# Weights cast to bf16 inside the DMA, in order of first use, with the conditioning projection first and in row form

## The chip, the cores and the metric

The kernel runs on all 8 cores of one Trainium2 chip. Every core does the same program on 2 of the 16 samples and no core talks to another. The metric is device time in microseconds of the slowest core. In code and profiles PE is TensorE, PEld the loading of its stationary operand, DVE is VectorE, ACT is ScalarE, POOL is GpSimd and SP is SyncE.

Such a program has two states. In the slow one the cores of one die, or of both, run at a lower granted TensorE clock and the time is some per cent longer (in one run one die stood at 0.84 and the other at 0.99). Where a number is given "by core", it is the median of the 8 cores of the one execution that was traced.

## The reference, cut to what matters

```python
shift, scale, gate = split(silu(c) @ w_mod + b_mod, 3)      # conditioning: (3, 1024) per sample
h  = rms_norm(x) * g_pre * (1 + scale) + shift              # needed before anything else
xa, ga, q, k, v, gb, gm = split(h @ w_in)                   # 1024 -> 5632
y_a = pool_mixer(xa) * silu(ga)                             # w_branch_a follows
y_b = windowed_attention(rope(q), rope(k), v, k_ctx, v_ctx) * silu(gb)   # w_branch_b follows
merged = sigmoid(gm_a) * (y_a @ w_branch_a) + sigmoid(gm_b) * (y_b @ w_branch_b)
out = x + gate * rms_norm(merged @ w_out) * g_post          # w_out: the last weight of a tile
```

Everything is fp32 in HBM. The kernel computes its large matmuls in bf16. The fp32 weights are 46 MB: 12.6 MB `w_mod`, 23.1 MB `w_in`, 10.5 MB for the two branch matrices and `w_out` (called `w_a`, `w_b`, `w_o` below).

Shift and scale are needed by the first tile's norm. The gate is needed only by the end of a tile.

## The kernel before

All weights stay in SBUF as bf16. A core first loads and converts all of them, then computes the conditioning, then works through 2 x (2 context + 32 latent) tiles of 128 tokens. The two start-up parts each end in a barrier, because their staging memory is used again by what follows.

```python
# part 1: stage every weight in fp32, cast it on DVE and ACT in turn   (5 staging buffers)
def load_cast(dst_ap, src_ap, n, dst_buf, mul_ap=None):
    si = cast_rr["s"] % NS
    E("sp", lambda e: e.dma_start(out=stg[si][:, 0:n], in_=src_ap), ...)              # L300
    if ci == 0:
        E("dve", lambda e: e.tensor_copy(out=dst_ap, in_=stg[si][:, 0:n]), ...)       # L308
    else:
        E("act", lambda e: e.activation(out=dst_ap, in_=stg[si][:, 0:n], func=AF.Copy), ...)  # L310
# ... w_tok, w_feat (= w_in), w_a, w_b, w_o, band and mask tables ...
tr.barrier()

# part 2: conditioning; six blocks of w_mod, [128, 8, 512] fp32 each, two buffers
for blk in range(6):
    if blk < 4:                      # shift, scale: column form, w_mod stationary
        for cc in range(4):
            for k in range(8):
                E("pe", matmul(out=psA[:, ch*4:(ch+1)*4],
                               lhsT=wst[wi][:, k, cc*128:(cc+1)*128], rhs=sc[:, k*4:(k+1)*4]))   # L375
    else:                            # gate: every row of the output is the same gate row
        for j in range(BPC):
            for k in range(8):
                E("pe", matmul(out=pg, lhsT=screp[j][:, k, :], rhs=wst[wi][:, k, :]))            # L384
# ... the gate rows go to a scratch tensor in HBM, 4 KB in one piece each, and come back broadcast ...
tr.barrier()
# part 3: the tiles
```

A helper keeps the order: each engine runs its own instructions strictly in program order, and an instruction waits for the producers of what it reads and the readers of what it overwrites. SP is the engine whose queue issues the DMAs here.

The softmax here doesn't subtract the row's maximum and nothing guards it: scores larger than these inputs give would overflow.

Of the kernel before, what the change touches and what calls it, by code (L numbers as in the profile page):

```python
# [13 lines left out]
D = 1024  # L14
# [4 lines left out]
NEG = -30000.0  # L19
HP = [0, 4, 1, 5, 2, 6, 3, 7, 8, 12, 9, 13, 10, 14, 11, 15]  # L20
# [149 lines left out]
def build_program(L, STOP=0):  # L170
    NT = L // 128
    nc = bass.Bass("TRN2", target_bir_lowering=False)
# [7 lines left out]
    wtok_d = din("w_tok", [D, 3072])  # L180
    wfeat_d = din("w_feat", [D, 2560])
    wa_d = din("w_a", [512, D])
    wb_d = din("w_b", [D, D])
    wout_d = din("w_o", [D, D])
    poolw_d = din("pool_w", [128, 512])
    wmod_d = din("w_mod", [D, 3072])
    bmodT_d = din("b_modT", [128, 16])
    bgate_d = din("b_gate", [1, D])
    gpreT_d = din("g_preT", [128, 8])
    gpost_d = din("g_post", [1, D])  # L190
# [24 lines left out]
    with es:  # L215
        def sb(name, shape, dt, stack=es):
            return stack.enter_context(nc.sbuf_tensor("s_" + name, list(shape), dt))

        Wtok = sb("Wtok", [128, 8, 3072], BF16)
        Wfeat = sb("Wfeat", [128, 8, 2560], BF16)  # L220
        Wa = sb("Wa", [128, 4, D], BF16)
        Wb = sb("Wb", [128, 8, D], BF16)
        Wo = sb("Wo", [128, 8, D], BF16)
# [54 lines left out]
        with ExitStack() as ps_:  # L278
            identf = sb("identf", [128, 128], F32, ps_)
            NS = 5  # L280
            stg = [sb(f"stg{i}", [128, 1536], F32, ps_) for i in range(NS)]
            pscl = sb("pscl", [128, 512], F32, ps_)
            sinkb = sb("sinkb", [128, 16], F32, ps_)

            E("pool", lambda e: e.memset(identf[:], 0.0), writes=[bf("identf")])
            E("pool", lambda e: e.affine_select(out=identf[:], in_=identf[:], pattern=[[-1, 128]],
                                                compare_op=ALU.not_equal, fill=1.0, base=0, channel_multiplier=1),
              reads=[bf("identf")], writes=[bf("identf")])
            E("pool", lambda e: e.tensor_copy(out=ident[:], in_=identf[:]), reads=[bf("identf")], writes=[bf("ident")])
            ld(pscl[:], pscale_d.partition_broadcast(128), "pscl")  # L290
            ld(sinkb[:], sink_d.partition_broadcast(128), "sinkb")

            cast_rr = {"i": 0, "s": 0}

            def load_cast(dst_ap, src_ap, n, dst_buf, mul_ap=None):
                si = cast_rr["s"] % NS
                cast_rr["s"] += 1
                sbuf_ = bf(f"stg{si}")
                s_ = dsem(f"d_stg{si}")
                E("sp", lambda e: e.dma_start(out=stg[si][:, 0:n], in_=src_ap), writes=[sbuf_], dma_sem=s_)  # L300
                if mul_ap is not None:
                    E("dve", lambda e: e.tensor_tensor(out=dst_ap, in0=stg[si][:, 0:n], in1=mul_ap, op=ALU.mult),
                      reads=[sbuf_, bf("pscl")], writes=[dst_buf])
                    return
                ci = cast_rr["i"] % 2
                cast_rr["i"] += 1
                if ci == 0:
                    E("dve", lambda e: e.tensor_copy(out=dst_ap, in_=stg[si][:, 0:n]), reads=[sbuf_], writes=[dst_buf])  # L308
                else:
                    E("act", lambda e: e.activation(out=dst_ap, in_=stg[si][:, 0:n], func=AF.Copy), reads=[sbuf_], writes=[dst_buf])  # L310

            for k in range(8):
                for h in range(2):
                    load_cast(Wtok[:, k, h * 1536:(h + 1) * 1536], wtok_d[k * 128:(k + 1) * 128, h * 1536:(h + 1) * 1536], 1536, bf("Wtok"))
            for k in range(8):
                for h in range(2):
                    load_cast(Wfeat[:, k, h * 1280:(h + 1) * 1280], wfeat_d[k * 128:(k + 1) * 128, h * 1280:(h + 1) * 1280], 1280, bf("Wfeat"))
            for k in range(4):
                load_cast(Wa[:, k, :], wa_d[k * 128:(k + 1) * 128, :], 1024, bf("Wa"))
            for k in range(8):  # L320
                load_cast(Wb[:, k, :], wb_d[k * 128:(k + 1) * 128, :], 1024, bf("Wb"))
            for k in range(8):
                load_cast(Wo[:, k, :], wout_d[k * 128:(k + 1) * 128, :], 1024, bf("Wo"))
            load_cast(view(Wp, 0, [[1, 512]]), poolw_d, 512, bf("Wp"), mul_ap=pscl[:])
            load_cast(view(band, 0, [[1, 1536]]), band_d[:, 0:1536], 1536, bf("band"))
            load_cast(view(band, 1536, [[1, 1024]]), band_d[:, 1536:2560], 1024, bf("band"))
            load_cast(view(maskb, 0, [[1, 256]]), mask_d, 256, bf("maskb"))
            E("act", lambda e: e.activation(out=esink[:], in_=sinkb[:], func=AF.Exp), reads=[bf("sinkb")], writes=[bf("esink")])
            tr.barrier()

        with ExitStack() as ps_:
            wst = [sb(f"wst{i}", [128, 8, 512], F32, ps_) for i in range(2)]
            cT = sb("cT", [128, 32], F32, ps_)
            th = sb("th", [128, 32], F32, ps_)
            sc = sb("sc", [128, 32], F32, ps_)
            screp = [sb(f"screp{j}", [128, 8, 128], F32, ps_) for j in range(BPC)]
            mT = sb("mT", [128, 64], F32, ps_)
            bmodT = sb("bmodT", [128, 16], F32, ps_)
            gpreT = sb("gpreT", [128, 8], F32, ps_)
            bgate = sb("bgate", [128, D], F32, ps_)  # L340
            gpost = sb("gpost", [128, D], F32, ps_)
            gtmp = sb("gtmp", [128, 512], F32, ps_)
            ggt1 = sb("ggt", [128, D], F32, ps_)
            ggt = [ggt1, ggt1]

            ld(cT[:], cT_d, "cT")
            def load_wmod(blk):
                wi = blk % 2
                E("sp", lambda e: e.dma_start(
                    out=wst[wi][:], in_=wmod_d[:, blk * 512:(blk + 1) * 512].rearrange("(k p) n -> p k n", p=128)),  # L350
                  writes=[bf(f"wst{wi}")], dma_sem=dsem(f"d_wst{wi}"))
            load_wmod(0)
            load_wmod(1)
            ld(bmodT[:], bmodT_d, "bmodT")
            ld(gpreT[:], gpreT_d, "gpreT")
            ld(bgate[:], bgate_d.partition_broadcast(128), "bgate")
            ld(gpost[:], gpost_d.partition_broadcast(128), "gpost")

            E("act", lambda e: e.activation(out=th[:], in_=cT[:], func=AF.Tanh, scale=0.5), reads=[bf("cT")], writes=[bf("th")])
            E("dve", lambda e: e.scalar_tensor_tensor(out=sc[:], in0=th[:], scalar=1.0, in1=cT[:], op0=ALU.add, op1=ALU.mult),  # L360
              reads=[bf("th"), bf("cT")], writes=[bf("sc")])
            E("dve", lambda e: e.tensor_scalar_mul(out=sc[:], in0=sc[:], scalar1=0.5), reads=[bf("sc")], writes=[bf("sc")])
            for j in range(BPC):
                E("dve", lambda e, j=j: e.tensor_copy(out=screp[j][:], in_=view(sc, j, [[4, 8], [0, 128]])),
                  reads=[bf("sc")], writes=[bf(f"screp{j}")])

            psA, psAb = next_bank()
            psG = [[next_bank() for nb in range(2)] for j in range(BPC)]
            for blk in range(6):
                wi = blk % 2  # L370
                if blk < 4:
                    for cc in range(4):
                        ch = blk * 4 + cc
                        for k in range(8):
                            E("pe", lambda e, wi=wi, cc=cc, ch=ch, k=k: e.matmul(  # L375
                                out=psA[:, ch * 4:(ch + 1) * 4], lhsT=wst[wi][:, k, cc * 128:(cc + 1) * 128],
                                rhs=sc[:, k * 4:(k + 1) * 4], start=(k == 0), stop=(k == 7)),
                              reads=[bf(f"wst{wi}"), bf("sc")], writes=[psAb], inc=(k == 7))
                else:
                    nb = blk - 4  # L380
                    for j in range(BPC):
                        pg, pgb = psG[j][nb]
                        for k in range(8):
                            E("pe", lambda e, wi=wi, j=j, k=k, pg=pg: e.matmul(  # L384
                                out=pg[:, :], lhsT=screp[j][:, k, :], rhs=wst[wi][:, k, :], start=(k == 0), stop=(k == 7)),
# [557 lines left out]
```

## Time and profile before

| | us |
|---|---|
| median of 4 runs | 2961.94 |
| fast runs | 2960.47, 2961.90, 2961.99 |
| one run in the slow state | 3227.13 |
| traced span of the slowest core | 2960.8 |
| first `w_o` matmul starts, by core | 290.8 (284.6 to 292.9) |
| from there to the end, by core | 2665.1 |

The page of the profile cuts the span into 40 equal slices of 74 us. A digit is the busy share of an engine in tenths; PEclk is the granted TensorE clock in tenths of full speed; DMA is the mean busy share of the core's 16 DMA engines.

```profile
span 2960.8 us, 80701 instructions; the slowest of 8 cores (2948.8 to 2960.8 us)
...
PE   0287999999999999999996999999999999999998
...
PEclk9998999999999999999998999999999999999999
DMA  9840000000000000000001000000000000000000
GB/s 316 252 115 30 32 32 32 17 32 32 32 17 32 32 32 24 25 32 32 32 16 53 17 32 32 20 29 32 32 27 22 32 32 32 17 32 32 32 24 16
```

TensorE is idle in the first slice and busy 90% or more in nearly every slice from the fifth on. The DMA engines are busy mainly at the start. So there is a start of some 300 us and a long TensorE-bound body.

The table of stretches gives, per stretch, the busy time of PE, PEld, DVE, ACT and POOL with their instruction counts, then clock, DMA share and GB/s:

```profile
core 7: us, PE busy (x) PEld busy (x) DVE busy (x) ACT busy (x) POOL busy (x), PEclk, DMA share, GB/s
...
60.00:80.00 20.00, 0.00 (x0) 0.00 (x0) 4.00 (x5) 6.64 (x6) 0.00 (x0) 1.00 1.00 334
...
160.00:180.00 20.00, 20.00 (x96) 20.00 (x95) 0.00 (x0) 0.00 (x0) 0.00 (x0) 1.00 0.59 173
...
200.00:220.00 20.00, 12.09 (x29) 5.04 (x27) 2.08 (x3) 0.00 (x0) 4.15 (x9) 0.85 0.11 27
```

```profile
304.00:346.00 42.00, 39.77 (x497) 27.94 (x496) 20.51 (x62) 18.52 (x36) 8.69 (x8) 1.00 0.10 32
346.00:388.00 42.00, 39.77 (x498) 27.93 (x496) 20.46 (x61) 18.52 (x36) 8.69 (x8) 1.00 0.09 31
```

While weights arrive, the DMA engines are saturated (1.00 at 334 GB/s) and the casts on DVE and ACT take a third of their time at most: they hide under the transfers. During the projection the DMA engines are half idle and TensorE is full. From 304 us on, a tile takes 42 us with 39.8 us of TensorE work. The Trainium skill ("HBM Reference", Specifications) gives about 358 GB/s per core when both cores of a pair are active; this trace shows somewhat less, 334.

The chain of waits, followed back from the end, lists start, length and what was waited for:

```profile
116.42 10.61 DMA s_wst<-w_mod
127.30 54.75 PE pb L375 x256
182.05 30.06 PE pb L384 x64
...
214.51 1.27 DMA gg_scr<-s_ggt
215.86 4.72 DMA s_xt<-ctx
...
294.25 1.89 PE pb L719 x8
```

The start is serial: weights to 115 us, projection to 212, tiles from 216, first output projection (L719, second half of its matmuls) at 294.

### The profile page before, as it was taken

To read this page: it belongs to the slowest core of one execution; us is meant where nothing else is said; L and a number is where in the kernel's file an instruction comes from. 1 tells how busy PE (TensorE), PEld (TensorE's weight loads), DVE (VectorE), ACT (ScalarE), POOL (GpSimd) and SP (SyncE) were. 2 spreads that over 40 slices of the span, in tenths; PEclk is the share of its full clock that TensorE was granted. 3 is DMA by queue.
4 is the path that set the end of the run, shared out by engine and by line. 5 is a ranking of instruction groups with operands and counts; after the bars stand their busy time and mean duration, and the time that the engine had idled before them with its cause. 6 is when DMAs were issued, how large, how long until landed. Compare 5 with 4: busy or idle time off the path is not lost.

```text
span 2960.8 us, 80701 instructions; the slowest of 8 cores (2948.8 to 2960.8 us)
## 1 busy us (share of the span) xinstructions
PE 2628.4 (89%) x31848; PEld 1851.0 (63%) x31848; DVE 1331.6 (45%) x3922; ACT 1225.9 (41%) x2338; POOL 564.8 (19%) x534
## 2 busy tenths in 40 slices
PE   0287999999999999999996999999999999999998
PEld 0264666666666666666664666666666666666666
DVE  1104444444444444444443444444444444444443
ACT  2103444444444444444443444444444444444443
POOL 0001222112221222122211122212221122112221
PEclk9998999999999999999998999999999999999999
DMA  9840000000000000000001000000000000000000
GB/s 316 252 115 30 32 32 32 17 32 32 32 17 32 32 32 24 25 32 32 32 16 53 17 32 32 20 29 32 32 27 22 32 32 32 17 32 32 32 24 16
DMA packets 44197, 128.82 MB, mean 44 GB/s; under 512 B 4786, under 2 KB 13106, under 8 KB 43828
## 3 DMA queue, kind: packets, MB, share of 16 engines
q1 hardware_dynamic: 43828, 123.66, 12.8%
q8 instruction: 261, 4.28, 0.6%
q14 instruction: 108, 0.88, 0.1%
HBM read 90.08 MB, written 33.56 MB: 42 GB/s over the span
## 4 chain that ended last, share of the span: by engine, by line
PE 59%; DVE 16%; issue 8%; ACT 7%; POOL 5%; DMA 4%; DVEq 1%; SPq 0%; POOLq 0%; ACTq 0%
PE pb L490 17%; PE pb L557 12%; PE pb L691 8%; DVE s_qrot L662 5%; PE pb L630 4%; ACT s_PT L638 4%; PE pb L719 4%; PE pb L635 3%; POOL s_mgT L710 3%; ACT s_xsb L458 2%; PE pb L681 2%; PE pb L375 2%; DVE s_mv L708 2%; DVE s_Gb L567 1%; PE pb L588 1%
## 5 line engine op out<-in xcount | busy, mean ns | idle before, releaser
L490 PE MATMUL pb<-s_Wtok,s_hT 128*128 128x512 bf16 x3104 | 715.1, 384 | 5.0 <-DVE s_hT L475 4.8
L638 ACT ACTIVATE s_PT<-pb 128x512 bf16<-128x512 f32 x1264 | 647.6, 612 | 162.6 <-PE pb L635 152.9
L557 PE MATMUL pb<-s_hT,s_Wfeat 128*128 128x128 bf16 x10240 | 623.6, 219 | 42.0 <-DVE s_small L655 32.6
L557 PEld LDWEIGHTS pb<-s_hT,s_Wfeat 128*128 128x128 bf16 x10240 | 580.1, 98 | 80.5 <-issue 80.5
L490 PEld LDWEIGHTS pb<-s_Wtok,s_hT 128*128 128x128 bf16 x3104 | 298.6, 99 | 364.3 <-issue 35.6
L699 ACT ACTIVATE s_Tm<-pb 128x512 bf16<-128x512 f32 x256 | 145.3, 591 | 459.4 <-PE pb L557 454.6
L710 POOL TENSOR_TENSOR s_mgT<-s_mu,s_mv 128x512 bf16<-128x512 f32 x128 | 162.0, 1265 | 650.6 <-DVE s_mv L708 650.6
L719 PE MATMUL pb<-s_Wo,s_mgT 128*128 128x512 bf16 x1024 | 241.7, 379 | 13.7 <-POOL s_mgT L710 13.7
L691 PE MATMUL pb<-s_ybT,s_Wb 128*128 128x128 bf16 x4096 | 253.0, 219 | 0.3
L691 PEld LDWEIGHTS pb<-s_ybT,s_Wb 128*128 128x128 bf16 x4096 | 235.0, 98 | 3.0 <-issue 0.6
L662 DVE SCALAR_TENSOR_TENSOR s_qrot<-pb,s_small,s_Gb 128x64 bf16<-128x64 f32 x1024 | 220.3, 277 | 28.5 <-DVE s_small L658 1.3
L461 POOL TENSOR_TENSOR s_small<-s_small,s_mh 128x1 f32<-128x1 f32 x68 | 37.2, 548 | 917.9 <-DVE s_small L460 917.9
L507 POOL TENSOR_TENSOR s_qrot<-s_rt 128x512 bf16<-128x512 f32 x128 | 162.0, 1265 | 256.5 <-DVE s_rt L503 256.5
L724 ACT ACTIVATE s_ttmp<-pb 128x512 bf16<-128x512 f32 x128 | 76.6, 598 | 303.9 <-PE pb L719 303.8
L737 POOL TENSOR_TENSOR s_xt<-s_xt,s_mu 128x512 f32<-128x512 f32 x128 | 162.2, 1267 | 134.0 <-DVE s_mu L734 132.9
L719 PEld LDWEIGHTS pb<-s_Wo,s_mgT 128*128 128x128 bf16 x1024 | 92.9, 97 | 134.3 <-issue 43.5
L500 DVE TENSOR_TENSOR s_rt<-pb,s_ropet 128x512 f32<-128x512 f32 (+1 forms) x192 | 115.2, 600 | 124.7 <-POOL s_qrot L507 96.9
L516 ACT ACTIVATE s_Vr<-pb 128x256 bf16<-128x256 f32 x64 | 24.6, 385 | 346.2 <-DVE s_rt L503 346.2
L375 PE MATMUL pb<-s_sc,s_wst 128*128 128x4 f32 x256 | 54.7, 354 | 127.3 <-DMA s_wst<-w_mod 127.3
L651 PE MATMUL pb<-s_Vr,s_PT 128*128 128x65 bf16 x3008 | 165.7, 193 | 0.0
L708 DVE SCALAR_TENSOR_TENSOR s_mv<-s_Tm,pb 128x512 f32<-128x512 bf16 x128 | 88.2, 689 | 170.1 <-PE pb L691 168.0
L734 DVE SCALAR_TENSOR_TENSOR s_mu<-pb,s_small,s_gg 128x512 f32<-128x512 f32 x128 | 96.1, 751 | 150.0 <-POOL s_xt L737 98.0
(92 smaller groups left out, 3058.6 us busy)
## 6 DMA issues: line engine op xcount, KB each, us to landing
s_xt<-x SPq DMA_DIRECT2D x64, 512.0 KB, 3.7
y<-s_xt SPq DMA_DIRECT2D x64, 512.0 KB, 2.6
s_stg<-w_tok SPq DMA_DIRECT2D x16, 768.0 KB, 10.4
s_wst<-w_mod SPq DMA_DIRECT2D x6, 2048.0 KB, 10.5
s_stg<-w_feat SPq DMA_DIRECT2D x16, 640.0 KB, 8.7
s_stg<-w_b SPq DMA_DIRECT2D x8, 512.0 KB, 7.9
s_stg<-w_o SPq DMA_DIRECT2D x8, 512.0 KB, 7.2
s_ropet<-rope SPq DMA_DIRECT2D x64, 64.0 KB, 3.5
```

What stands on the lines that cost most here:

```text
L490: E("pe", lambda e, k=k: e.matmul(out=pb[:, :], lhsT=hT[h3][:, k, :], rhs=Wtok[:, k, nb * 512:(nb + 1) * 512], start=(k == 0), stop=(k == 7)),
L507: E(add_eng, lambda e: e.tensor_tensor(out=out_t[:, out_off:out_off + n], in0=rt1[:, 0:n], in1=rt2[:, 0:n], op=ALU.add), reads=[bf("rt1"), ...
L557: E("pe", lambda e, pb=pb, c4=c4, ch=ch, k=k: e.matmul(out=pb[:, c4 * 128:(c4 + 1) * 128], lhsT=Wfeat[:, k, ch * 128:(ch + 1) * 128], rhs= ...
L638: E("act", lambda e, sbk=sbk, jb=jb, g=g: e.activation(out=PT2[g % 2][:, jb, :], in_=sbk[:, :], func=AF.Exp, scale=0.125), reads=[sbb], wr ...
L651: E("pe", lambda e, r=r, jb=jb, rv=rv: e.matmul(out=ob[:, r * 128:r * 128 + 65], lhsT=PT2[g % 2][:, jb, r * 128:(r + 1) * 128], rhs=rv, st ...
L662: E("dve", lambda e, r=r, co=co: e.scalar_tensor_tensor(out=yb[:, co:co + 64], in0=ob[:, r * 128:r * 128 + 64], scalar=small[:, 12 + r:13 ...
L691: E("pe", lambda e, c4=c4, cd=cd, k=k: e.matmul(out=pbk[:, c4 * 128:(c4 + 1) * 128], lhsT=Wb[:, k, cd * 128:(cd + 1) * 128], rhs=ybT[:, k, ...
L699: E("act", lambda e: e.activation(out=Tm[:, half, :], in_=pgm[:, :], func=AF.Tanh, scale=0.5), reads=[pgmb], writes=[bf(f"Tm{half}")])
L708: E("dve", lambda e: e.scalar_tensor_tensor(out=mv[:], in0=Tm[:, 1, :], scalar=1.0, in1=pbk[:, :], op0=ALU.add, op1=ALU.mult), reads=[bf(" ...
L710: E("pool", lambda e: e.tensor_tensor(out=view(mgT, rd * 512, [[1, 512]]), in0=mu[:], in1=mv[:], op=ALU.add), reads=[bf("mu"), bf("mv")], ...
L719: E("pe", lambda e, pb=pb, nb=nb, k=k: e.matmul(out=pb[:, :], lhsT=mgT[:, k, :], rhs=Wo[:, k, nb * 512:(nb + 1) * 512], start=(k == 0), st ...
L737: E("pool", lambda e, nb=nb: e.tensor_tensor(out=xs_[slot][:, nb * 512:(nb + 1) * 512], in0=xs_[slot][:, nb * 512:(nb + 1) * 512], in1=mu[ ...
```

## The change

The intent is to let loads, projection and first tiles overlap.

- The weights go straight into resident bf16 tiles by casting DMAs, issued from GpSimd, in the order of first use. No staging, no casts on DVE and ACT, no barriers.
- `w_in` is cut into 11 blocks of 2 MB with a tile name of their own, so that a matmul waits only for its block. The host passes the weights in this block layout, with source rows of 16 KB (32 KB for `w_b` and `w_o`) instead of 4 to 6 KB.
- The projection runs first, in row form: the conditioning vectors are stationary (4 columns) and `w_mod` streams through as 512 columns. The result is a [4, 512] row that four small fp32 transposes turn back into columns.
- The gate's two blocks run in the middle of the first latent tile. `w_b` and `w_o` share memory with the two `w_mod` buffers, so they are loaded only after these blocks.

The core of the diff (cut):

```diff
+        def load_cast(dst, src, bname, reads=()):
+            E("pool", lambda e: e.dma_start(out=dst, in_=src), reads=reads, writes=[bf(bname)], dma_sem=...)
+        def mod_block(blk):
             for k in range(8):
-                for h in range(2):
-                    load_cast(Wtok[:, k, h * 1536:(h + 1) * 1536], wtok_d[...], 1536, bf("Wtok"))
...
+                E("pe", lambda e, k=k: e.matmul(out=pg[0:4, :], lhsT=sc[:, k * 4:(k + 1) * 4], rhs=wmf[blk % 2][:, k, :], ...))
+            E("dve", lambda e: e.tensor_copy(out=mr[:], in_=pg[0:4, :]), ...)
+            for cc in range(4):
+                E("pe", lambda e, cc=cc, ch=ch: e.matmul(out=psA[:, ch * 4:(ch + 1) * 4], lhsT=mr[:, cc * 128:(cc + 1) * 128],
+                                                         rhs=identf[0:4, 0:4], start=True, stop=True), ...)
...
+        def start_b():
+            load_w(0, reads=[bf("wmf0")])          # not before w_mod block 2 has landed
+            for blk in range(1, 8):
+                load_w(blk)
+            load_cast(Wa ...); load_cast(band ...); load_cast(maskb ...)
+            load_w(8); load_w(9)
+            for blk in range(2, 4):
+                mod_block(blk)
+                load_wmod(blk + 2, "pool")
...
+        def start_gate():                           # called inside the first latent tile
+            for blk in range(4, 6):
+                mod_block(blk)
+            load_cast(flat2(wmf[0]), wb_d, "wmf0")
+            load_w(10)
+            load_cast(flat2(wmf[1]), wout_d, "wmf1")
...
+                        return e.dma_start(out=AP(ggs_d.tensor, j * D, [[1, 128], [128, 8]]), in_=view(ggT, j, [[4, 8]]))
-            tr.barrier()
...
+        start_a(first_loads)       # w_mod 0 to 3, projection blocks 0 and 1
+        front(work[0])             # first norm
+        start_b()
```

The line with `ggs_d` stores the gate rows from column layout, so it moves single fp32 elements: 1024 pieces of 4 bytes a sample.

## The prediction

> **What bounds it now.** From 304 us on, the table of stretches shows the same 42 us per tile with TensorE busy 39.8 us: TensorE-bound, and the change leaves that code alone. Before that, the timeline and the chain of waits show a serial start: weights staged until 115 us (DMA share about 1, 333 GB/s; casts hidden under it), a barrier, the conditioning projection (first w_mod block lands at 127.3; 256 fp32 matmul passes of 214 ns, 54.7 us; then 64 passes, 30.1 us), gate rows, a second barrier; the first tile is loaded at 215.9 and transposed at 224.2. The first output projection (w_o) starts at 292 us.
>
> **What changes.** The same 46 MB of fp32 weights are read: 46 MB / 333 GB/s = 138 us is the floor at today's rate. Row form: each of six w_mod blocks takes 16 passes of 512 columns (timeline: one every 0.86 us for the first five us, then every 0.43) = 7 us warm, 14 cold, plus about 2.5 us of copy and small transposes; four blocks are needed before any tile.
>
> My schedule (estimates from those durations and 6.3 us per 2 MB):
> - w_mod 0 and 1 land at about 11 and 17 us; scale and shift ready at 55 to 65 us.
> - W0 is held until w_mod 2 lands, about 28 us; then W0 to W9, Wa and band stream: W9 at about 107, w_mod 4 and 5 at 115 and 121.
> - Today 61 us pass from the first transposes (224.2) to the ybT transposes of tile 0 (285.0); so TensorE gets there at 116 to 126.
> - Then two gate blocks, about 20 us; only then are Wb, W10, Wo asked for (10.5 MB, 31 us): first output projection at 160 to 170 us instead of 292.
>
> Saved: about 125 to 132 us, all on the critical path, if a casting transfer reads as fast as the plain ones.
>
> **The doubt.** No casting DMA is in this trace. The Trainium skill ("DMA: Bandwidth & Descriptors", SWDGE vs HWDGE vs iDMA) says a cast during DMA can only be issued from GpSimd, whose software writes the descriptors. If the 34 MB of casts read at 230 instead of 333 GB/s, they take 45 us more; at 150, most of the gain is gone. GpSimd's queue is also in order: if descriptor space fills, the second tile's norm waits. Mixing these in: predicted saving 118 us.
>
> **Prediction: 2844 us, range 2810 to 2905.** Chances: faster by over 2% 0.88, within 2% 0.11, slower 0.01.
>
> **What would show it.**
> - Stretches: DMA share near 1 from about 5 to 150 us, first bf16 hT matmuls at 55 to 80 us, 42 us per tile unchanged later: the whole gain is in when the first w_o projection starts.
> - Groups by line: staging casts gone; 96 fp32 passes of 512 columns for 320.
> - DMA list: W blocks on a GpSimd queue, landing about 6 us apart; 9 or more apart means the cast rate is the limit.
> - Waits: TensorE waits for W blocks and, after the gate blocks, 5 to 20 us for Wb, and again for W10 or Wo.
>
> **What would make it wrong.** A slow cast in the DMA; GpSimd stalled in descriptor writing; the gate rows written as 4-byte pieces and read back late, holding the first output; steady tiles changed by another bank rotation or granted clock.

## The result, and the profile after

| | before | after |
|---|---|---|
| median, us | 2961.94 | 2854.26 |
| range of the fast runs, us | 2960.47 to 2961.99 | 2854.14 to 2854.77 |
| first bf16 matmul on `hT`, by core, us | 224.3 | 56.4 |
| first `w_o` matmul, by core, us | 290.8 (284.6 to 292.9) | 181.0 (175.1 to 187.3) |
| from there to the end, by core, us | 2665.1 | 2667.4 |

The ratio is 0.9639, 95% interval 0.9623 to 0.9654. A ratio here is the mean time of one kernel's fast runs over that of the other's fast runs of the same rounds, so it is not quite the ratio of the medians quoted.

`hT` is the normed tile, transposed, so its first matmul marks the start of the tiles. The whole gain, 108 us, lies ahead of the first output projection (110 us earlier by core). The body is as long as before to within 3 us.

```profile
span 2852.8 us, 79877 instructions; the slowest of 8 cores (2841.3 to 2852.8 us)
...
PE   6769999999999999999978999999999999999998
...
PEclk8879999999999999999989999999999999999999
DMA  8860000000000000000010000000000000000000
GB/s 212 185 97 25 26 33 33 17 33 33 19 32 33 33 18 33 33 17 33 32 56 9 26 33 33 18 33 33 19 32 33 33 18 33 33 17 33 33 25 17
```

GB/s looks lower than before at the same DMA share. The trace counts a packet by what it writes: a W block is listed as 1024 KB although 2 MB are read. From 60 to 100 us the packets of GpSimd's queue, all casts, add up to 6.19 MB written and those of SP's queue, plain x and rope tiles, to 1.18 MB. So 2 x 6.19 + 1.18 = 13.6 MB were read in 40 us, about 340 GB/s.

The table of stretches of the same core (columns as before):

```profile
24.00:37.00 13.00, 11.34 (x34) 3.59 (x35) 1.59 (x5) 0.83 (x2) 0.12 (x1) 0.87 0.61 172
...
60.00:100.00 40.00, 29.38 (x125) 12.81 (x126) 16.75 (x55) 9.29 (x16) 5.45 (x6) 0.74 1.01 185
...
136.00:142.00 6.00, 5.07 (x19) 1.66 (x17) 0.85 (x2) 0.00 (x0) 1.13 (x2) 1.00 0.00 0
...
165.00:186.00 21.00, 6.12 (x73) 6.11 (x75) 2.71 (x9) 0.60 (x1) 1.26 (x1) 0.66 0.80 88
```

```profile
280.00:322.00 42.00, 39.67 (x495) 28.00 (x496) 20.51 (x62) 18.50 (x36) 8.70 (x8) 1.00 0.08 28
```

The stream of weights is full from 37 to 136 us. It has a hole before it (0.61), an empty stretch after it (0.00), and a last piece that moves slowly (88 GB/s). A steady tile is as it was.

The chain of waits of the same core shows what held the first output projection (L318 projection passes, L619 attention mask, L703 output projection):

```profile
13.88 9.82 PE pb L318 x16
...
34.48 12.14 DMA s_wmf<-w_mod
...
100.77 11.29 another core or an unknown queue
112.20 1.01 PE pb L619 x8
...
132.51 6.97 PE pb L318 x16
...
141.42 6.97 PE pb L318 x16
...
148.93 36.42 DMA s_wmf<-w_o
185.34 0.62 issue
185.97 5.50 PE pb L703 x15
```

The unnamed 11.29 us are the wait for the mask table, which landed at 112.06 us, eleventh in its queue. Then the two gate blocks. Then 36 us in which TensorE gets a little work done but ends up waiting for `w_o`. The first projection block takes 9.82 us and the two of the gate 6.97 each: TensorE starts at half clock. The Trainium skill ("TensorE: Matmul & The Clock Gate", Part 1) describes this start, and the trace agrees: passes of 512 columns follow each other every 0.86 us at first and every 0.43 us later. Blocks 1 and 3, which begin after a pause, are slow at first again (8.67 and 8.74 us; the recorded clock is 0.5 at 26.3 to 29.7 and 46.8 to 50.2 us).

GpSimd's timeline (start, length, what, and in brackets its idle time before) shows when the weights were asked for:

```profile
36.88 0.55 POOL L444 TENSOR_TENSOR s_small<-s_small,s_mh 128x1 f32<-128x1 f32 x1 [34.22 <-DVE s_small L443]
37.44 4.43 POOL L303 DMA_DIRECT2D s_W<-w_in  x8
...
140.02 0.59 POOL L303 DMA_DIRECT2D s_wmf<-w_b  x1 [10.84 <-PE pb L318]
140.61 0.54 POOL L303 DMA_DIRECT2D s_W<-w_in  x1
148.93 0.53 POOL L303 DMA_DIRECT2D s_wmf<-w_o  x1 [7.78 <-PE pb L318]
```

W0 was to wait for `w_mod` block 2, which landed at 33.17 us. It was issued at 37.44, right behind the first norm's `pow` on the same in-order queue. That one waited for DVE, whose queue was still in projection block 1.

### The profile page after: what moved, and what is told of

Read it like the earlier page. It is cut to its first block, busy times and chain, and to the rows that moved or that the text cites. A ratio compares the mean times of both kernels' runs of the same rounds, so it can differ in the third digit from the quotient of the medians.

```text
span 2852.8 us, 79877 instructions; the slowest of 8 cores (2841.3 to 2852.8 us)
## 1 busy us (share of the span) xinstructions
PE 2597.4 (91%) x31542; PEld 1802.2 (63%) x31672; DVE 1309.6 (46%) x3899; ACT 1190.3 (42%) x2311; POOL 570.2 (20%) x548
## 4 chain that ended last, share of the span: by engine, by line
PE 51%; DVE 20%; issue 10%; ACT 8%; POOL 7%; DMA 2%; DVEq 1%; another core or an unknown queue 0%; POOLq 0%; ACTq 0%; SPq 0%
PE pb L541 13%; PE pb L474 10%; PE pb L675 8%; DVE s_qrot L646 6%; PE pb L614 5%; PE pb L703 4%; ACT s_PT L622 4%; PE pb L619 3%; POOL s_mgT L694 3%; POOL s_xt L721 3%; ACT s_xsb L441 2%; PE pb L665 2%; DVE s_krot L491 2%; DVE s_mu L718 2%; DVE s_Gb L551 2%
## 5 line engine op out<-in xcount | busy, mean ns | idle before, releaser
L474 PE MATMUL pb<-s_W,s_hT 128*128 128x512 bf16 x3038 | 701.3, 384 | 9.8 <-DVE s_hT L458 6.3
L541 PE MATMUL pb<-s_hT,s_W 128*128 128x128 bf16 x10240 | 625.2, 219 | 45.0 <-DVE s_small L639 31.1
L541 PEld LDWEIGHTS pb<-s_hT,s_W 128*128 128x128 bf16 x10240 | 581.6, 98 | 83.7 <-issue 83.7
L474 PEld LDWEIGHTS pb<-s_W,s_hT 128*128 128x128 bf16 x3104 | 298.3, 99 | 365.5 <-issue 36.9
L675 PE MATMUL pb<-s_ybT,s_wmf 128*128 128x128 bf16 x4096 | 254.8, 220 | 6.6 <-DMA s_wmf<-w_b 6.6
L703 PE MATMUL pb<-s_wmf,s_mgT 128*128 128x512 bf16 x960 | 229.8, 381 | 31.1 <-DMA s_wmf<-w_o 14.2
L675 PEld LDWEIGHTS pb<-s_ybT,s_wmf 128*128 128x128 bf16 x4096 | 236.9, 98 | 9.0 <-issue 6.7
L444 POOL TENSOR_TENSOR s_small<-s_small,s_mh 128x1 f32<-128x1 f32 x68 | 37.4, 550 | 957.9 <-DVE s_small L443 957.9
L703 PEld LDWEIGHTS pb<-s_wmf,s_mgT 128*128 128x128 bf16 x1024 | 93.5, 98 | 149.6 <-issue 59.8
L484 DVE TENSOR_TENSOR s_rt<-pb,s_ropet 128x512 f32<-128x512 f32 (+1 forms) x192 | 115.2, 600 | 125.4 <-POOL s_qrot L491 97.6
L619 PE MATMUL pb<-s_maskb,s_ident 128*128 128x128 bf16 x1984 | 154.2, 221 | 11.4 <-DMA s_maskb<-mask 11.4
```

Source lines behind the costliest of these rows:

```text
L474: E("pe", lambda e, k=k: e.matmul(out=pb[:, :], lhsT=hT[h3][:, k, :], rhs=W[:, wblk, k, :], start=(k == 0), stop=(k == 7)), reads=[bf(f"hT ...
L541: E("pe", lambda e, pb=pb, c4=c4, k=k: e.matmul(out=pb[:, c4 * 128:(c4 + 1) * 128], lhsT=W[:, wblk, k, c4 * 128:(c4 + 1) * 128], rhs=hT[h3 ...
L619: E("pe", lambda e, sbk=sbk, mk=mk, r=r: e.matmul(out=sbk[:, r * 128:(r + 1) * 128], lhsT=ident[:], rhs=maskb[:, mk, :], start=False, stop ...
L675: E("pe", lambda e, c4=c4, cd=cd, k=k: e.matmul(out=pbk[:, c4 * 128:(c4 + 1) * 128], lhsT=Wb[:, k, cd * 128:(cd + 1) * 128], rhs=ybT[:, k, ...
L703: E("pe", lambda e, pb=pb, nb=nb, k=k: e.matmul(out=pb[:, :], lhsT=mgT[:, k, :], rhs=Wo[:, k, nb * 512:(nb + 1) * 512], start=(k == 0), st ...
```

## The experiments

Theory: the gain is overlap, and the cast in flight is worth nothing alone but makes the overlap possible. Rivals: taking the casts off DVE and ACT is the gain; or the row form is. Later experiments ask why the first output projection came at 181 us and not at the 160 to 170 of my schedule.

Medians are of fast runs. Chips differ, so the unchanged "after" was run again beside the last group, where it took 2861.4 us (ratio 0.9649).

### cast_only: the kernel before with casting DMAs

```diff
 def load_cast(dst_ap, src_ap, n, dst_buf, mul_ap=None):
-    E("sp", dma_start(out=stg[si][:, 0:n], in_=src_ap)); cast on DVE or ACT
+    E("pool", lambda e: e.dma_start(out=dst_ap, in_=src_ap), writes=[bf(nm)], dma_sem=dsem("d_" + nm))
```

> The kernel before with one part of the change alone: the weight loads are casting transfers into the resident tiles, issued from GpSimd; order, barriers and projection as before. Theory (the gain is overlap; the staging casts were hidden under the transfers and the cast in flight is only what makes overlap possible): the weight phase, today 115 us, stays between 105 and 118 us, total 2950 to 2965 us. Rival (taking the casts off DVE and ACT is itself the gain): the weight phase is at least 30 us shorter, total below 2930 us. If casting transfers were slow, the total would be above 2990 us.

Measured: one fast run, 2963.26 us, beside 2961.96 us for before (three of its four runs fell in the slow state, so there is no interval). In the trace the last table landed at 115.2 us; before, at 114.5. The casts are gone from DVE and ACT and nothing came of it. The first rival, which expected 30 us or more, falls, though there is one fast run only. Casting transfers also read as fast as plain ones did, over the whole load.

### row_only: the kernel before with the row form

```diff
-            for blk in range(6): column form for blocks 0 to 3, replicated rows for 4 and 5
+            for blk in range(6): 8 matmuls [4, 512], copy, 4 small transposes, bias   (as in the change)
-            gate rows stored as [1, 1024]
+            gate rows stored from columns: out=AP(ggs_d.tensor, j * D, [[1, 128], [128, 8]])
```

> The kernel before with the row form of the projection alone (96 passes of 512 columns and small transposes instead of 320 passes), loads, order and barriers as before. From the changed kernel's trace one block takes about 10.7 us with its copy and transposes, so six take 60 to 66 us instead of 85: total 2935 to 2945 us, 17 to 27 us gained. In this serial kernel the projection is on the critical path in full. Rival (the row form is the main gain): more than 50 us.

Measured: 2963.65 us, ratio 1.0011 (0.9988 to 1.0034). I expected 17 to 27 us and got none. The chain of waits of this kernel shows where they went:

```profile
185.16 0.20 DVE s_ggT L383
185.40 0.04 issue
185.44 16.54 DMA gg_scr<-s_ggT
202.01 0.04 issue
202.05 10.14 DMA gg_scr<-s_ggT
```

The projection took 57 us where it had taken 85. Then two stores of 4 KB each, in 4-byte pieces, took 26.7 us, with no other transfer in flight. Before, such a store stood in the chain with 1.27 us.

### row_only_rows: the same with contiguous gate rows

```diff
+                if blk >= 4:      # stay in rows: (row + bias) * 32 * g_post on DVE, no transposes
+                    continue
-        out=AP(ggs_d.tensor, j * D, [[1, 128], [128, 8]]), in_=view(ggT, j, [[4, 8]])
+        out=ggs_d[j:j + 1, h * 512:(h + 1) * 512], in_=mrow[h][j:j + 1, :]
```

> row_only again (row form in the kernel before), which gained nothing: the projection was 30 us shorter but two stores of the gate rows in 4-byte pieces then took 26.6 us on the critical path. Here the gate rows are stored as contiguous rows. If the stores were the whole loss, the first output projection starts at 258 to 264 us (before 285 to 293), total 2932 to 2940 us. If the gain is still missing, total above 2955 us.

Measured: 2931.8 us, ratio 0.9890 (0.9873 to 0.9906), first `w_o` matmul at 262.5 us by core (257.0 to 266.0). So the stores were the whole loss, and the row form is worth about 1% in a kernel where the projection stands alone on the critical path.

### all_landed_first: the changed kernel without overlap with tiles

```diff
-        start_a(first_loads)
-        front(work[0])
-        start_b()
+        start_a(first_loads); start_b(); start_gate()      # gate blocks here, not in the first tile
+        tr.barrier()
+        front(work[0])
...
-                load_wmod(blk + 2, "pool")
+                load_wmod(blk + 2, "sp")      # w_mod 4 and 5
```

> The changed kernel with one part undone: a barrier keeps the first token tile waiting until the whole projection is done and every weight has landed; casts in flight, row form, order of loads kept. Weights land by about 155 to 165 us; from the first norm to the first output projection 68 to 75 us follow, as in the kernel before (224 to 292 us). So the first output projection starts at 225 to 240 us instead of 186, total 2893 to 2910 us: of the gain of 108 us some 40 to 55 come from running tiles while weights arrive, the rest from running the projection while weights arrive. Rival (overlap with tiles is worth little since the DMA stream binds anyway): total within 10 us of the changed kernel's 2854.

Measured: 2926.7 us, ratio 0.9878 (0.9860 to 0.9895), first `w_o` matmul at 255.4 us by core. The direction is as expected, but 15 to 30 us later: `w_o` landed at 175 to 185 us instead of 155 to 165. The order of loads was not quite kept: by SP's queue w_mod 4 and 5 landed at 67 and 82 us (core 0) instead of 129 and 136, ahead of most weights. landed_rows has this edit too, so the two can be compared.

### landed_rows: the same with contiguous gate rows

The edit is that of row_only_rows, in this kernel.

> all_landed_first again (no tile until everything has landed), with contiguous gate rows. There the weights landed at 175 to 185 us instead of the 155 to 165 expected, with the 4-byte stores in flight from 87 us on. If those stores slowed the stream, w_o lands here by 155 to 165 us, the first output projection starts at 228 to 237 us, total 2897 to 2909 us (against 2926). If the stream was slow for another reason, w_o still lands after 172 us and the total is above 2918 us.

Measured: 2907.9 us, ratio 0.9809 (0.9793 to 0.9825); `w_o` landed at 161.0 to 166.9 us, first `w_o` matmul at 238.5 us by core. The total lies in my range, landing and first matmul up to 2 us above theirs; the question is answered. The stretches of all_landed_first and then of landed_rows (last number: GB/s written):

```profile
80.00:100.00 20.00, 10.51 (x24) 2.52 (x24) 1.05 (x3) 0.00 (x0) 0.53 (x1) 0.68 1.02 168
100.00:120.00 20.00, 0.00 (x0) 0.00 (x0) 0.00 (x0) 0.00 (x0) 0.00 (x0) 0.50 1.01 109
120.00:140.00 20.00, 0.00 (x0) 0.00 (x0) 0.00 (x0) 0.00 (x0) 0.00 (x0) 0.50 1.06 117
```

```profile
80.00:100.00 20.00, 11.20 (x26) 2.02 (x24) 2.72 (x4) 0.00 (x0) 1.58 (x3) 0.99 1.01 183
100.00:120.00 20.00, 0.00 (x0) 0.00 (x0) 0.00 (x0) 0.00 (x0) 0.00 (x0) 0.50 1.02 168
120.00:140.00 20.00, 0.00 (x0) 0.00 (x0) 0.00 (x0) 0.00 (x0) 0.00 (x0) 0.50 1.06 174
```

Both show a DMA share of 1. With the 4-byte stores in flight (issued at 94 us, the last landed at 186) the engines moved a third less. So 8 KB of tiny pieces slowed a stream of some 20 MB, and the DMA share did not show it.

### column_form: the row form undone for blocks 0 to 3

```diff
+            if blk < 4:            # 64 passes with w_mod stationary, 4 columns each, then the bias
+                ...matmul(out=psA[:, ch*4:(ch+1)*4], lhsT=wmf[blk % 2][:, k, cc*128:(cc+1)*128], rhs=sc[...])
+                return
```

> The changed kernel with the row form undone for the four blocks that the first tile needs (64 passes of 214 ns each = 13.7 us a block instead of about 10.7). Scale and shift come some 11 us later (69 instead of 57.5 us). Theory: this is absorbed, since TensorE waits 11.4 us for the mask table at 100.8 to 112.2 us; the first output projection moves by less than 4 us and the total is 2852 to 2859 us. Rival (the projection is on the critical path here too): 10 us or more slower, above 2863 us.

Measured: 2873.4 us, ratio 0.9702 (0.9681 to 0.9723). My theory of absorption failed. Scale and shift came 14 us later and the first `w_o` matmul 9 us later by core (190.4; the control below, on a third chip, stands at 186.0). The mask table was not a fixed point to wait for: it landed at 116 to 120 us instead of 108 to 112, because the weights were asked for later. GpSimd's timeline of column_form:

```profile
42.41 0.55 POOL L456 TENSOR_TENSOR s_small<-s_small,s_mh 128x1 f32<-128x1 f32 x1 [39.75 <-DVE s_small L455]
42.97 4.42 POOL L303 DMA_DIRECT2D s_W<-w_in  x8
```

### column_free: the same, with the weights asked for ahead of the norm

```diff
         start_a(first_loads)
+        stream()                  # W0 to W9, Wa, band, mask: taken out of start_b
         front(work[0])
```

> column_form again (old projection form for the four first blocks in the changed kernel), which came out 12 to 17 us slower against my expectation. In its trace the weights were asked for at 43 to 47 us instead of 37, because their issue stands behind the first norm in GpSimd's queue and that norm behind projection block 1 on VectorE. Here the weights are asked for ahead of that norm; all else as in column_form. New theory (the form cost time only through that late request): the stream is as early as in the control, mask lands at 106 to 113 us, the first output projection is within 4 us of the control, total within 6 us of it (2853 to 2861 us). Rival (the longer projection itself is on the critical path): total stays at 2866 to 2874 us.

Measured: 2863.9 us, ratio 0.9660 (0.9645 to 0.9674), beside 2861.4 us for the unchanged kernel; first `w_o` matmul at 189.5 us by core against 186.0. GpSimd's timeline of column_free:

```profile
39.04 4.43 POOL L303 DMA_DIRECT2D s_W<-w_in  x8 [36.39 <-DMA s_wmf<-w_mod]
...
46.01 0.69 POOL L458 TENSOR_TENSOR s_small<-s_small,s_mh 128x1 f32<-128x1 f32 x1
```

Now the longer projection costs 2.5 us, although scale and shift came 20 us later than in the control. This fits the new theory, that the projection's length is absorbed once the weights are not asked for behind it, but does not prove it: column_form ran on another chip, without a control beside it. By ratio column_free is faster (0.9660 against 0.9702, intervals apart), and its slowest core starts earlier (195.4 instead of 199.0 us); by the median of the cores the first `w_o` matmul is only 1 us earlier (189.5 against 190.4). The mask landed at 113 to 119 us, later than I had written: w_mod block 3 was asked for later too and went through the same engines.

### after_again: control

> Control: the changed kernel unaltered, on the chip of the three runs beside it. Total 2853 to 2858 us, ratio to before 0.963 to 0.965, first output projection at 175 to 187 us by core.

Measured: 2861.4 us, ratio 0.9649 (0.9629 to 0.9668), first `w_o` matmul at 179.3 to 190.0 us. The total is 3 us above my range, the ratio is in it. This chip is slightly slower than that of the first measurement, for both kernels.

### mask_first: the mask table asked for second

```diff
             load_w(0, reads=[bf("wmf0")])
+            load_cast(view(maskb, 0, [[1, 256]]), mask_d, "maskb")
...
-            load_cast(view(maskb, 0, [[1, 256]]), mask_d, "maskb")
```

> The changed kernel, but the small mask table is asked for right after W0 instead of after ten larger transfers. The 11.4 us that TensorE waits for it (100.8 to 112.2 us) go. If that wait is worth what it lasts, the total falls by about 11 us to 2843 us. My theory: the gate blocks then wait for their own w_mod blocks, which land at 130.5 and 135.8 us in the same stream (gate block 4 starts at 132.4 today), so the first output projection moves by 1 to 3 us and the total is 2850 to 2854 us.

Measured: 2857.3 us, ratio 0.9633 (0.9602 to 0.9665). The table landed at 50 to 55 us, the 11 us wait is gone and the total did not fall: it is 3 us above my range, and the ratio is that of the changed kernel (0.9639 and 0.9649 in its two measurements). The first `w_o` matmul starts at 183.0 us by core. The time after the wait ran into the w_mod blocks 4 and 5, which land at 126 to 137 us as before.

### halves: `w_b` and `w_o` in two transfers each

```diff
-            load_cast(flat2(wmf[0]), wb_d, "wmf0")          # source rows of 32 KB
+            load_half(0, wb_d, 0); load_half(0, wb_d, 1)      # source rows of 16 KB
```

> The changed kernel, but Wb and w_o are each loaded by two casting transfers with source rows of 16 KB, like the other weight blocks, instead of one with rows of 32 KB. Theory B (row length): Wb needs 13 to 14 us instead of 17.8 after its issue, w_o about 13 instead of 19.8, the first output projection starts 8 to 12 us earlier, total 2842 to 2847 us. Theory A (the 4-byte gate store is to blame): Wb changes by less than 2 us, w_o by less than 3 us, total 2851 to 2855 us.

Measured: 2858.8 us, ratio 0.9636 (0.9609 to 0.9663). The second half of `w_o` landed at 172 to 193 us; in the changed kernel all of it landed at 175 to 187. The length of the rows is not what slowed the end. Here the start of the first `w_o` matmul misleads: by core it comes at 174.2 us, 9 earlier than in mask_first on the same chip, for a total that is no better. It needs only the first half of `w_o`; TensorE then waits 3 to 10 us for the second.

### gate_rows: contiguous gate rows in the changed kernel

The edit is again that of row_only_rows.

> The changed kernel, but the two gate blocks stay in row form and are stored as rows of 2 KB instead of 4-byte pieces (no small transposes for them). In the row_only run the two 4-byte stores took 16.5 and 10.1 us with nothing beside them, and in all_landed_first the weight packets took 0.95 to 1.06 us instead of 0.65 to 0.70 while such a store was in flight. Theory A (the 4-byte store slows the last weight transfers): the last one, w_o, lands 19.8 us after the one before it in the changed kernel; here 13 to 16 us, and the first output projection starts 5 to 9 us earlier, total 2845 to 2849 us (ratio to before 0.961 to 0.962). Theory B (long rows of the source slow Wb and w_o): w_o still takes 18 us or more, total gains no more than 2 us for the missing transposes, 2852 to 2854 us.

Measured: 2848.6 us, ratio 0.9601 (0.9578 to 0.9624). On the same chip mask_first and halves, which cost what the changed kernel does, took 2857.3 and 2858.8: 9 to 10 us gained, and no fast run of one overlaps with one of the other (at most 2850.0 here, at least 2855.4 there). Up to 2 us of it may be the small transposes that are gone. `w_o` landed 11.0 to 14.3 us after the block ahead of it, instead of 15.9 to 20.8. The time from asking for `w_b` to the landing of `w_o` is 34.9 us by core instead of 42 (44.6 in mask_first). In the chain of waits the 36.42 us for `w_o` have become 28:

```profile
151.46 28.06 DMA s_wmf<-w_o
```

Theory A holds.

### stream_first: all of it together

```diff
         first_loads()
+            stream()        # gated on w_mod block 1, ahead of the norm; mask second
...
-                load_wmod(blk + 2, "pool")
+                load_wmod(blk + 2, "sp")     # w_mod 4 and 5 right behind 2 and 3
...
+                if b == 0:                    # gate block 4 after context tile 0, block 5 after tile 1;
+                    start_gate(i)             # each is followed by its share of w_b, W10, w_o in halves
+   contiguous gate rows; the first latent x tile is asked for ahead of the weights
```

> Everything together: mask first, halves, contiguous gate rows, the weight stream started when w_mod block 1 has landed instead of behind the first norm, w_mod 4 and 5 loaded right after 2 and 3, the gate blocks run between the first tiles, so that Wb, W10 and w_o follow in the stream without a hole (today no weight moves from 135.8 to 140 us and the last 10 MB are asked for only after 140 us). 46 MB at 333 GB/s end at about 145 to 155 us; the first output projection starts at 150 to 162 us instead of 175 to 187, total 2823 to 2836 us (ratio 0.953 to 0.957). If the stream is not what binds, less than 10 us are gained.

Measured: 2833.5 us, ratio 0.9556 (0.9529 to 0.9584), some 24 us below mask_first and halves on the same chip, and the fastest kernel. The stretch in which the changed kernel moved nothing is filled (DMA share 1.04):

```profile
136.00:142.00 6.00, 5.06 (x91) 3.95 (x88) 4.69 (x16) 2.50 (x6) 0.00 (x0) 1.00 1.04 174
```

Going by gate_rows, some 9 us of the 24 are due to the gate rows; which of the other edits brought the remaining 15 was not tested. The first `w_o` matmul starts at 157.4 us by core (155.2 to 159.8); it needs only the first half of `w_o`, so from there to the end it takes 2669.3 us, 2 to 5 more than in the kernels that load `w_o` whole. It starts although scale and shift are ready later than in the changed kernel: the first `hT` matmul comes at 70.8 us instead of 56.4.

## Why the prediction was right

The predicted time was 2844 us with a range of 2810 to 2905; 2854 us were measured. The number owes something to luck: the schedule alone said 125 to 132 us saved, and the 118 came from an allowance for a slow cast, which was not needed. Three mis-sized terms, below, took what it had set aside and 10 us more. The mechanism was right, point by point:

- "TensorE-bound, and the change leaves that code alone": from the first output projection to the end 2665.1 us before and 2667.4 after.
- "The whole gain is in when the first w_o projection starts": 110 us earlier by core, 108 us in the total.
- "First bf16 hT matmuls at 55 to 80 us": 53.9 to 59.3.
- "The doubt", a slow cast: not so. W blocks landed 5.6 to 7.6 us apart on the traced core (from 74.65 us for W3 to 101.22 for W7, 6.64 on average: 316 GB/s read). Plain w_mod blocks in the same queue landed 5.9 and 5.3 us apart. cast_only shows the same at the level of the whole load.
- "5 to 20 us for Wb, and again for W10 or Wo": TensorE waited 6.6, 4.2 and 14.2 us.
- "GpSimd stalled in descriptor writing": no. The thirteen issues behind the first norm took 0.5 to 0.7 us each and returned long before their data landed.

The time came out 10 us over, and the first output projection at 181 us by core instead of 160 to 170. Three terms of the schedule were mis-sized:

- "W0 is held until w_mod 2 lands, about 28 us". It was asked for at 37.4. Of that, 5 us are w_mod 2 itself (33.2), and 4 us the queue: W0 stood behind the first norm, and that behind projection block 1 on DVE. The stream then took 87 us to W9 instead of the planned 79, since blocks were 6.6 us apart and 1.7 MB of x and rope tiles shared the engines. W9 landed at 124.6, not 107.
- "DMA share near 1 from about 5 to 150 us": 0.61 before the stream and 0.00 from 136 to 142 us. `w_b` and `w_o` could not be asked for there, since they need the memory of the gate's w_mod blocks; W10 has memory of its own, but stood behind `w_b` in GpSimd's queue.
- "Wb, W10, Wo: 10.5 MB, 31 us". 42 us by core. About 7 us of the difference (9 against mask_first, on the same chip) are the 4-byte gate stores, which gate_rows shows by removing them.

I had named those stores as a risk because they might be read back late. They were. On the traced core, the slowest, 3.5 us were to spare (the broadcast landed at 190.05 us, its first reader began at 193.57). But on cores 1, 2, 4 and 7, which had `w_o` first, VectorE sat idle for 3.2 to 6.2 us until the broadcast landed. What the stores did besides, slowing the transfers beside them, I had not thought of.

Where the 108 us come from, by the start of the first `w_o` matmul:

```
kernel                                        first w_o matmul, us (median of cores)
before                                                    290.8
row form alone                          (row_only)        288.2
row form, gate rows contiguous          (row_only_rows)   262.5
and weights loaded during projection    (landed_rows)     238.5
and tiles run while weights arrive      (gate_rows)       176.0
the change as made, with 4-byte stores                    181.0
and the other edits of stream_first     (stream_first)    157.4
```

The largest step is the overlap with tiles, about 60 us. The step to landed_rows also holds the casts in flight, the new order and the block layout, which were not taken apart further. The lines come from different chips, which adds an uncertainty of a few us (the control stood at 186.0 instead of 181.0).

What stays open: why `w_b` takes 13 to 18 us for 4 MB in the changed kernel, differing by core, when 12.6 would follow from 333 GB/s. Neither row length nor gate stores explain it: it took 13 to 18 us in halves and in gate_rows 13 to 17. One pattern is clear: in each of the 20 pairs of neighbouring cores (0 and 1, 2 and 3, ...) of after, after_again, mask_first, halves and gate_rows, the core that asked earlier, by its own clock, had `w_b` within 12.7 to 14.8 us and the other within 16.1 to 19.1; why is not shown. And why 4-byte pieces slow other transfers: the traces show longer packets beside them (0.95 to 1.06 us instead of 0.65 to 0.70 in all_landed_first), but not the cause.

## What to carry to other kernels

A wait in the chain is worth only what lies between it and the next wait: the 11 us for the mask were worth nothing, while the moment at which the stream was asked for, which no wait names, was worth several us by the ratios of column_form and column_free. In a load-bound start, look for holes in the DMA share and ask which in-order queue or shared buffer kept the next request back. And store small results as contiguous rows: 8 KB in 4-byte pieces cost 27 us alone, or a third of the bandwidth of the core's other transfers while in flight.

## What the Trainium skill lacked or had wrong

- "DMA: Bandwidth & Descriptors", SWDGE vs HWDGE vs iDMA: it says that a cast during DMA must be issued from GpSimd (the trace agrees: the casts are in the queue `q0 software_dynamic`), but gives no rate for a casting transfer. Measured here: 2 MB of fp32 into bf16 every 6.6 us, 316 GB/s of source, with all 8 cores running the program; a plain 2 MB block in the same queue took 5.3 to 5.9 us.
- Same page, Specifications: below 512 B it names a read-modify-write, but the page gives no size of the loss for a store of 4-byte pieces and no effect on others. Measured: 1024 pieces of 4 bytes took 16.5 and 10.1 us to land with nothing beside them, and with them in flight the casting stream fell from 168 to 109 GB/s written at an unchanged DMA share of about 1.
- Same page, "Issuing engines are not separate DMA queues": it says that transfers interleave, whichever engine issued them. They do (plain and casting ones land in turn here), but it gives no price for it, and a late small load pays: the first latent x tile from SP, 512 KB, took 20.7 us to land beside the stream, against a median of 3.6 us later.
- "TensorE: Matmul & The Clock Gate" gives no durations for fp32 matmuls. Measured: the trace lists two passes for each fp32 matmul (16 for the 8 of a block); with 4 columns and a 128-column fp32 weight a pass took 214 ns, with 512 columns 0.43 us (0.86 at half clock).
